# Weight chunks of a hybrid decoder layer: low parts by ScalarE's negative and an accumulating DMA, low-part matmuls at the end of each tile

## The chip, the cores and the metric

The kernel runs on one core of one Trainium2 chip. The metric is the device time in microseconds (us) of one execution.

## What is computed

The reference is one decoder layer on 512 tokens of width 1024, in float32. A conditioned norm gives `h`; one wide GEMM `z = h @ w_in` feeds three causal mixers, whose outputs are projected up, gated and merged; a squared-ReLU MLP follows.

```python
h = rms_norm(x, g_norm1[l]) * (1.0 + sc1) + sh1
x = x + gt1 * hybrid_mixer(h, w_in[l], ...)
h = rms_norm(x, g_norm2[l]) * (1.0 + sc2) + sh2
x = x + gt2 * (jnp.square(jax.nn.relu(h @ w_mlp1[l])) @ w_mlp2[l])
...
z = h @ w_in
merged = jax.nn.sigmoid(ga) * y_a + jax.nn.sigmoid(gbr) * y_b + jax.nn.sigmoid(gc) * y_c
return merged @ w_out
```

`y_a` is a gated MLP over chunks of 128 tokens, `y_b` a matrix memory with forget gates (mLSTM), `y_c` a sparse attention of eight heads with a compressed, a selected and a window branch, each times its projection up.

## The kernel before, in words

Every GEMM runs in split precision. A float32 operand is written as the exact sum of a high and a low part, both of type float32r, and a product takes three matmuls: high by high, low by high, high by low. The rows of activations are split once (`hh`, `hl`), the weights stream.

Weights come in chunks of 128 partitions by up to 1024 columns (512 KB). `chunk` (line 105) loads one by a DMA that SyncE issues (SP in the profile) into `w_raw` (three buffers), ScalarE (ACT) rounds it to `w_hi` (line 109, two buffers), and one engine subtracts, `w_lo = w_raw - w_hi` (line 110, two buffers): GpSimd (POOL) where `pool_lo` is true, VectorE (DVE) elsewhere. So the low part of a chunk goes into the buffer that the chunk two places earlier has used.

```python
raw = load(src, cols)
hi = stream.tile([P, D], F32R, name="w_hi", tag="hi")[:, :cols]
lo = stream.tile([P, D], F32R, name="w_lo", tag="lo")[:, :cols]
V.tensor_copy(hi, raw) if dve_hi else A.copy(hi, raw)
(G if pool_lo else V).tensor_tensor(lo, raw, f(hi), op=ALU.subtract)
```

`pool_lo` is true for 53 chunks: the 8 of 768 columns of the first GEMM (lines 193 to 254), 2 column tiles of compressed keys and values and 3 chunks of small columns (two of 864 columns, one of 576; lines 415 to 422), the 12 of `early_fill` (lines 851 to 894), 12 for each of two calls of `merge` (8 gate tiles of `zt`, 4 of the projection up; lines 822 to 850) and 4 for the output gate of the mLSTM (`ztok`, lines 289 to 306). 84 others go by DVE.

The program has these stages. In the first (to about 64 us) the shift and scale of the norm are made: `early_mod` (line 202) loads rows of the modulation weights, `ada_raw`, and reduces them, three quarters on DVE (line 210) and one on POOL (line 207) with ACT; `early_h` (line 218) makes a column tile of `h`. The first GEMM takes the tiles as they come: for each of 8 chunks 6 matmuls of `w_hi` by `hh`, then 6 pairs of `w_hi` by `hl` and `w_lo` by `hh` (lines 244 to 254). Then come the compressed keys, the small columns and, from about 96 us, `early_fill`. The attention (about 125 to 256 us) is an order written out by hand for TensorE (PE), ACT and DVE, in which a step of `early_fill` follows each block of scores. From 256 us the gated MLP runs beside the first merge, until about 480 us the mLSTM beside two merges, and after that no chunk has `pool_lo`. Outside the stretches written by hand a scheduler orders each engine's queue from its own estimate of times.

`mm3` (line 113) issues the three matmuls of a pair of tiles one after the other, so that a low weight part is read at every third matmul (`L114`, `L115`, `L116`). `zt` makes a column tile of `z` from one chunk (24 matmuls of 512 columns), `ztok` a token block from two (48 of 256 columns each).

Of the kernel before, what the change touches and what calls it, by code (L numbers as in the profile page):

```python
# [11 lines left out]
ALU = mybir.AluOpType  # L12
# [30 lines left out]
# columns of the per-partition vector pack  # L43
V_C, V_G1, V_G2, V_SH1, V_SC1, V_SH2, V_SC2, V_CB, V_CW, V_PEK, V_PEV, V_LNG, V_LNB, V_NG, V_N = (
    0, 8, 16, 24, 32, 40, 48, 56, 64, 96, 128, 160, 164, 168, 172)
# columns of the row pack that is broadcast over the partitions
R_GB, R_BS = 0, 8
# order of the column tiles that are computed transposed
# [12 lines left out]
def trunk_kernel(ctx: ExitStack, tc: tile.TileContext, x, vecs, rows, late_rows, ada1, w_ada,  # L61
# [15 lines left out]
    def page(tag, name, dt=F32, width=S):  # L77
        """a tile of 512 columns (and a little) that outlives the step that writes it"""
        t = work.tile([P, 520 if tag == "kv" else S], dt, name=name, tag=tag, bufs=SLOTS[tag])
        return t[:, :width]  # L80
# [10 lines left out]
    def split(hi, lo, src, scale=None):  # L91
        """src (times scale) as the exact sum of two float32r parts"""
# [12 lines left out]
    def chunk(src, cols=D, pool_lo=False, dve_hi=False):  # L105
# [4 lines left out]
        (G if pool_lo else V).tensor_tensor(lo, raw, f(hi), op=ALU.subtract)  # L110
# [6 lines left out]

    def rstd_of(ss, n, name, scale=1.0 / D):
        """1/sqrt(ss*scale + EPS)"""
        r = small.tile([P, n], F32, name=name)  # L120
        V.tensor_scalar(r, ss, scale, EPS, op0=ALU.mult, op1=ALU.add)
        G.tensor_tensor(r, r, mhalf[:, 0:r.shape[1]], op=ALU.pow)
        return r
# [4 lines left out]
    # ---------------------------------------------------------------- loads and constants of the start  # L128
# [24 lines left out]
    # the condition as a row on all partitions  # L153
# [7 lines left out]
    # ---------------------------------------------------------------- first norm, transposed and split  # L161
# [20 lines left out]
    # 1/rms of the tokens as a row on all partitions  # L182
# [9 lines left out]
    def early_mod(j):  # L192
        """shift and scale of a column tile: the first by the tensor engine, the others along rows of the
        transposed weights"""
# [61 lines left out]
    # ---------------------------------------------------------------- constants of the mixers  # L256
# [23 lines left out]
    # ---------------------------------------------------------------- GEMM helpers on h^T  # L280
    def zt(n, pool_lo=False, tag="mm"):
        """column tile n of z, transposed: [128 columns, S]"""
        wh, wl = chunk(w_zt[n], D, pool_lo)
        ps = bank(tag, "zt")
        for k in range(KD):
            mm3(ps, wh[:, tsl(k)], wl[:, tsl(k)], hh[k], hl[k], k == 0, k == KD - 1)
        return ps

    def ztok(n, evac, pool_lo=True):
        """256 columns of z in token layout: two banks of two blocks; a step for each chunk of weights"""  # L290
        ps = [bank("mm", "ztok") for _ in range(2)]
        for c in range(2):
            wh, wl = chunk(w_tok[n * 2 + c], D, pool_lo)
            for tb in range(NT):
                o = ps[tb // 2][:, (tb % 2) * 256:(tb % 2) * 256 + 256]
                for kk in range(4):
                    k = 4 * c + kk
                    ws_ = slice(kk * 256, (kk + 1) * 256)
                    T.matmul(o, hh[k][:, tsl(tb)], wh[:, ws_], start=k == 0 and tb % 2 == 0, stop=False)
                    T.matmul(o, hl[k][:, tsl(tb)], wh[:, ws_], start=False, stop=False)  # L300
                    T.matmul(o, hh[k][:, tsl(tb)], wl[:, ws_], start=False, stop=k == KD - 1 and tb % 2 == 1)
# [6 lines left out]
    # ---------------------------------------------------------------- NSA operands  # L308
# [32 lines left out]
    # compressed keys and values: the windows, gathered by pairs of positions  # L341
    vc = []
    # per group: 32 columns of the high parts, 32 of the low ones
# [20 lines left out]
    def halves(name, src, eng):  # L364
        """16 blocks of 64 columns, each beside its rest: both float32r parts in one operand of 128 columns"""
# [42 lines left out]
    # values of the two dense branches, mLSTM gates, NSA gates: token layout  # L408
# [6 lines left out]
    for c, (k0, k1) in enumerate(((0, 3), (3, 6), (6, 8))):  # L415
        wh, wl = chunk(w_small[:, k0 * 288:k1 * 288], (k1 - k0) * 288, pool_lo=True)
        for tb in range(NT):
            for k in range(k0, k1):
                ws_ = slice((k - k0) * 288, (k - k0 + 1) * 288)
                T.matmul(sm[tb][:, :288], hh[k][:, tsl(tb)], wh[:, ws_], start=k == 0, stop=False)  # L420
                T.matmul(sm[tb][:, :288], hl[k][:, tsl(tb)], wh[:, ws_], start=False, stop=False)
                T.matmul(sm[tb][:, :288], hh[k][:, tsl(tb)], wl[:, ws_], start=False, stop=k == KD - 1)
# [11 lines left out]
    # ---------------------------------------------------------------- NSA attention  # L434
# [4 lines left out]
    def cmp_scores(g):  # L439
        """scores and weights of the compressed branch for the four heads of group g, in steps"""  # L440
# [43 lines left out]
    def scores(n, tb):  # L484
        """a block of rows of the scores, their bias and their maximum"""
# [24 lines left out]
    def scale(n, t0, t1):  # L510
        """exp(s - max) of blocks t0 to t1 times gate / sum"""
# [10 lines left out]
    def turn(n, sb):  # L522
        """the weights of a block of keys, transposed"""
# [14 lines left out]
    def apply(n, sb):  # L538
        """values of a block of keys times their weights"""
# [32 lines left out]
    # ---------------------------------------------------------------- gMLP  # L572
# [12 lines left out]
    def gelu2(ts):  # L585
        """twice the gelu, in place"""
# [45 lines left out]
    # ---------------------------------------------------------------- mLSTM  # L632
    bias_t = const.tile([P, 10, 4], F32, name="d_bias")
    em = const.tile([P, NT, 4], F32, name="em")
    # a row per head, the low parts 32 rows below the high ones
# [5 lines left out]
    def mlstm_gates():  # L641
# [23 lines left out]
        # sums of the log forget gates within blocks of 128, the running stabilizer  # L665
# [37 lines left out]
    def evac_mv(half):  # L703
        def ev(tb, ps):
            # two heads to a page: high part, one, zero, low part
# [14 lines left out]
    def conv(i, ps):  # L720
        """column tile i of q and k after the conv, silu and scale: two float32r parts"""
# [99 lines left out]
    # ---------------------------------------------------------------- merge of the gated branches  # L821
# [3 lines left out]
    def merge(b, yh, yl):  # L825
        """adds branch b of the three, two column tiles at a time: gates, then the projection up"""
# [531 lines left out]
```

## Time and profile before

| what | value |
|---|---|
| median of 3 runs | 973.5 us (972.73 to 974.67) |
| span of the profiled execution | 973.2 us, 0.3 us below the median |
| PE busy | 933.4 us, 96% |
| DVE, ACT, POOL busy | 612.2, 402.4, 193.7 us |
| DMA engines, queue of SP | 35.0% of 16 engines' span, 110.91 MB |

The profile gives no time of its own for the profiled execution beside its span. It lists, for each engine, groups of instructions by line of the kernel with their count, busy time and mean duration, the idle time before them and what ended it. Matmuls overlap: one of 512 columns shows about 0.39 us, and the next starts 0.23 us later. The granted clock is the share of TensorE's full speed (2.4 GHz) that was granted; 0.5 of it is the lower of two levels (1.2 GHz).

### The profile page before, as it was taken

The page shows a single profiled execution, that of the slowest core. Times are in us where ns is not written, and L with a number is a line of the kernel's source. Part 1 is how long each engine was busy: PE and PEld are TensorE (multiplying, and loading weights), DVE is VectorE, ACT ScalarE, POOL GpSimd, SP SyncE. Part 2 cuts the span into 40 slices and gives each one's busy share as a digit, 9 for nine tenths or more (in the row PEclk, how much of TensorE's full clock was granted, in tenths as well). Part 3 has the DMA queues.
Part 4 walks back from the last instruction along what each step waited for, and adds up shares of the span by engine and source line. Part 5 has one row for each costly group of instructions (what it writes and reads, how often), then busy time and mean ns, then how long its engine had stood idle before and what let it go on. Part 6 is the DMA issues. An engine that isn't in the chain of part 4 may idle for free.

```text
span 973.2 us, 12531 instructions
## 1 busy us (share of the span) xinstructions
PE 933.4 (96%) x4688; PEld 778.5 (80%) x4688; DVE 612.2 (63%) x1186; ACT 402.4 (41%) x789; POOL 193.7 (20%) x130
## 2 busy tenths in 40 slices
PE   7789998998979999999999999999999999999996
PEld 5569986797867888888977778888888888888886
DVE  6977679776497456556688799766424254442435
ACT  5355565765533444443333344544321223432221
POOL 5565423333343122123300003000000000000001
PEclk9899999998999999999999999999999999999998
DMA  9733210110222222222568864354333333223222
GB/s 328 229 118 116 66 44 26 40 44 26 84 65 87 87 86 88 70 82 89 172 211 274 258 251 119 92 182 128 94 100 91 104 89 107 87 89 106 87 87 87
DMA packets 36285, 111.72 MB, mean 115 GB/s; under 512 B 4160, under 2 KB 4352, under 8 KB 36224
## 3 DMA queue, kind: packets, MB, share of 16 engines
q1 hardware_dynamic: 36224, 110.91, 35.0%
q8 instruction: 37, 0.61, 0.3%
q14 instruction: 24, 0.20, 0.1%
HBM read 108.80 MB, written 2.10 MB: 114 GB/s over the span
## 4 chain that ended last, share of the span: by engine, by line
PE 75%; DVE 15%; DMA 6%; issue 2%; ACT 1%; SPq 0%; POOL 0%; POOLq 0%; DVEq 0%; ACTq 0%
PE tok L1086 6%; PE tok L1088 6%; PE tok L1087 6%; PE m L114 6%; PE m L116 6%; PE m L115 6%; PE zt L116 5%; PE zt L114 5%; PE zt L115 5%; DMA ada_raw<-in_w_ada 4%; DVE ada_raw L210 2%; PE pv L553 2%; PE pT L528 2%; PE ztok L887 2%; PE ztok L886 2%
## 5 line engine op out<-in xcount | busy, mean ns | idle before, releaser
L109 ACT CAST w_hi<-w_raw 128x1024 fp32r<-128x1024 f32 (+2 forms) x137 | 141.4, 1032 | 256.6 <-PE tok L1087 98.0
L110 DVE TENSOR_TENSOR w_lo<-w_raw,w_hi 128x1024 fp32r<-128x1024 f32 x84 | 103.8, 1236 | 171.1 <-ACT w_hi L109 171.1
L110 POOL TENSOR_TENSOR w_lo<-w_raw,w_hi 128x1024 fp32r<-128x1024 f32 (+3 forms) x53 | 125.1, 2360 | 242.9 <-ACT w_hi L109 240.3
L116 PE MATMUL zt<-h_hi,w_lo 128*128 128x512 f32 x304 | 121.1, 398 | 4.0 <-POOL w_lo L110 2.3
L114 PE MATMUL zt<-h_hi,w_hi 128*128 128x512 f32 x304 | 122.3, 402 | 0.5 <-ACT w_hi L109 0.5
L115 PE MATMUL zt<-h_lo,w_hi 128*128 128x512 f32 x304 | 119.9, 394 | 0.0
L114 PE MATMUL m<-h_hi,w_hi 128*128 128x512 f32 (+1 forms) x272 | 104.1, 383 | 0.0
L116 PE MATMUL m<-h_hi,w_lo 128*128 128x512 f32 (+1 forms) x272 | 103.7, 381 | 0.0
L115 PE MATMUL m<-h_lo,w_hi 128*128 128x512 f32 (+1 forms) x272 | 103.6, 381 | 0.0
L1087 PE MATMUL tok<-w_hi,f_lo 128*128 128x512 f32 (+1 forms) x232 | 88.6, 382 | 0.0
L1086 PE MATMUL tok<-w_hi,f_hi 128*128 128x512 f32 (+1 forms) x232 | 88.6, 382 | 0.0
L1088 PE MATMUL tok<-w_lo,f_hi 128*128 128x512 f32 (+1 forms) x232 | 84.4, 382 | 0.0
L116 PEld LDWEIGHTS zt<-h_hi,w_lo 128*128 128x128 f32 x304 | 57.6, 190 | 17.3 <-DVE w_lo L110 2.8
L114 PEld LDWEIGHTS zt<-h_hi,w_hi 128*128 128x128 f32 x304 | 57.6, 189 | 12.1 <-ACT w_hi L109 0.7
L115 PEld LDWEIGHTS zt<-h_lo,w_hi 128*128 128x128 f32 x304 | 57.6, 190 | 10.7
L1228 POOL TENSOR_TENSOR o_g<-x,gfin 128x512 f32<-128x512 f32 x1 | 1.3, 1297 | 311.0 <-DVE x L1132 311.0
L115 PEld LDWEIGHTS m<-h_lo,w_hi 128*128 128x128 f32 x272 | 51.2, 188 | 10.8
L116 PEld LDWEIGHTS m<-h_hi,w_lo 128*128 128x128 f32 x272 | 51.1, 188 | 10.8
L114 PEld LDWEIGHTS m<-h_hi,w_hi 128*128 128x128 f32 x272 | 51.1, 188 | 10.7
L1087 PEld LDWEIGHTS tok<-w_hi,f_lo 128*128 128x128 f32 x232 | 43.6, 188 | 8.6
L1086 PEld LDWEIGHTS tok<-w_hi,f_hi 128*128 128x128 f32 x232 | 43.6, 188 | 8.5
L1088 PEld LDWEIGHTS tok<-w_lo,f_hi 128*128 128x128 f32 x232 | 43.6, 188 | 8.4
(390 smaller groups left out, 2022.3 us busy)
## 6 DMA issues: line engine op xcount, KB each, us to landing
w_raw<-in_w_m SPq DMA_DIRECT2D x64, 512.0 KB, 3.5
w_raw<-in_w_zt SPq DMA_DIRECT2D x38, 512.0 KB, 3.3
ada_raw<-in_w_ada SPq DMA_DIRECT2D x24, 512.0 KB, 5.1
ada_raw<-in_ada SPq DMA_DIRECT2D x32, 256.0 KB, 4.9
w_raw<-in_w_tok SPq DMA_DIRECT2D x12, 512.0 KB, 3.3
w_raw<-in_w_up SPq DMA_DIRECT2D x12, 512.0 KB, 3.5
w_raw<-in_w_out SPq DMA_DIRECT2D x8, 512.0 KB, 4.8
w_raw<-in_w_ada SPq DMA_DIRECT2D x8, 512.0 KB, 3.9
```

Of the source, the lines that this page charges most:

```text
L109: V.tensor_copy(hi, raw) if dve_hi else A.copy(hi, raw)
L110: (G if pool_lo else V).tensor_tensor(lo, raw, f(hi), op=ALU.subtract)
L114: T.matmul(ps, ah, bh, start=first, stop=False)
L115: T.matmul(ps, ah, bl, start=False, stop=False)
L116: T.matmul(ps, al, bh, start=False, stop=last)
L210: V.scalar_tensor_tensor(raws[q], raws[q], 1.0, condb[:, (q % 2) * 512:(q % 2) * 512 + 512], op0=ALU.mult, op1=ALU.mult, accum_out=s4[:, q ...
L528: T.transpose(tp[:, tsl(tb)], sb_[:, boff(tb) + c0:boff(tb) + c0 + P], ident)
L553: T.matmul(acc[:, c0:], vv, p_[:, c0:], start=False, stop=last and p_ is t[-1])
L886: T.matmul(o, hh[k][:, tsl(tb)], wh[:, ws_], start=k == 0 and tb % 2 == 0, stop=False)
L1086: T.matmul(p_, ah_, wh, start=k == 0, stop=False)
L1087: T.matmul(p_, al_, wh, start=False, stop=False)
L1088: T.matmul(p_, ah_, wl, start=False, stop=k == 2 * n - 1)
```

## The change

Where `pool_lo` is true, `w_lo` is no longer a subtraction on POOL. ACT writes the negative of `w_hi` into `w_lo`, and POOL issues a DMA that adds the weights from DRAM to it. `w_raw` is then read by ACT alone, and the same weights are read from DRAM twice. `mm_hi` is new; in `zt`, `ztok`, the small columns, `merge` and `early_fill` the matmuls that read `w_lo` come after all those of the tile that read `w_hi` (in `merge` for both column tiles of a chunk, whose two banks are now taken together). The pairs of the first GEMM stay as they were. In `early_fill` the evacuation of the first bank pair moves to the last sixth of the second chunk. Comments and docstrings are gone, so lines are numbered anew.

```diff
@@ chunk
-        (G if pool_lo else V).tensor_tensor(lo, raw, f(hi), op=ALU.subtract)
+        if pool_lo:
+            A.activation(lo, f(hi), AF.Copy, scale=-1.0)
+            G.dma_start(lo, src, accum_op=ALU.add)
+        else:
+            V.tensor_tensor(lo, raw, f(hi), op=ALU.subtract)
+    def mm_hi(ps, ah, bh, bl, first):
+        T.matmul(ps, ah, bh, start=first, stop=False)
+        T.matmul(ps, ah, bl, start=False, stop=False)
@@ zt
         for k in range(KD):
-            mm3(ps, wh[:, tsl(k)], wl[:, tsl(k)], hh[k], hl[k], k == 0, k == KD - 1)
+            mm_hi(ps, wh[:, tsl(k)], hh[k], hl[k], k == 0)
+        for k in range(KD):
+            T.matmul(ps, wl[:, tsl(k)], hh[k], start=False, stop=k == KD - 1)
...
@@ merge
             wh, wl = chunk(w_up[b][jp], D, pool_lo)
+            ups = [bank(UP_BANK[b][u], "up") for u in range(2)]
+            for u in range(2):
+                for k in range(4):
+                    mm_hi(ups[u], wh[:, tsl(u * 4 + k)], yh[k], yl[k], k == 0)
             for u in range(2):
                 j = 2 * jp + u
-                ps = bank(UP_BANK[b][u], "up")
+                ps = ups[u]
                 for k in range(4):
-                    mm3(ps, wh[:, tsl(u * 4 + k)], wl[:, tsl(u * 4 + k)], yh[k], yl[k], k == 0, k == 3)
+                    T.matmul(ps, wl[:, tsl(u * 4 + k)], yh[k], start=False, stop=k == 3)
...
@@ early_fill
-                for k in range(KD):
-                    mm3(ps, wh[:, tsl(k)], wl[:, tsl(k)], hh[k], hl[k], k == 0, k == KD - 1)
-                    if k < KD - 1:
+                mms = [(wh, k, o) for k in range(KD) for o in (hh, hl)] + [(wl, k, hh) for k in range(KD)]
+                for n_, (w_, k, o) in enumerate(mms):
+                    T.matmul(ps, w_[:, tsl(k)], o[k], start=n_ == 0, stop=n_ == len(mms) - 1)
+                    if n_ % 3 == 2 and n_ < len(mms) - 1:
                         yield
...
```

`ztok`, the small columns and the token units of `early_fill` are rewritten in the same way. Three places show how the queues move. In the rows the names carry buffer numbers.

POOL's queue in the first stage, before:

```order
L110 TENSOR_TENSOR w_lo_219<-w_raw_216,w_hi_218 128x768
L207 TENSOR_TENSOR ada_raw_259<-ada_raw_259,condb_119 128x512
L110 TENSOR_TENSOR w_lo_268<-w_raw_265,w_hi_267 128x768
L207 TENSOR_TENSOR ada_raw_308<-ada_raw_308,condb_119 128x512
L110 TENSOR_TENSOR w_lo_317<-w_raw_314,w_hi_316 128x768
L207 TENSOR_TENSOR ada_raw_357<-ada_raw_357,condb_119 128x512
```

and the same place of POOL's queue now:

```order
L113 DMA w_lo_219<-in_w_early 128x768
L217 TENSOR_TENSOR ada_raw_260<-ada_raw_260,condb_119 128x512
L113 DMA w_lo_269<-in_w_early 128x768
L217 TENSOR_TENSOR ada_raw_310<-ada_raw_310,condb_119 128x512
L217 TENSOR_TENSOR ada_raw_360<-ada_raw_360,condb_119 128x512
L113 DMA w_lo_319<-in_w_early 128x768
```

Each subtraction has become the issue of a DMA; the third chunk's issue has moved behind a further product of the modulation.

ACT's queue in the first stage, before, from the second chunk on:

```order
L109 CAST w_hi_267<-w_raw_265 128x768
L208 ACTIVATE ada_raw_259,ada_s_271<-ada_raw_259 128x512
L109 CAST w_hi_316<-w_raw_314 128x768
L232 ACTIVATE h_hi_289<-h_tmp_288,ab_285 128x512
L208 ACTIVATE ada_raw_308,ada_s_320<-ada_raw_308 128x512
L232 ACTIVATE h_hi_338<-h_tmp_337,ab_334 128x512
L208 ACTIVATE ada_raw_357,ada_s_369<-ada_raw_357 128x512
L109 CAST w_hi_365<-w_raw_363 128x768
```

and the same place now:

```order
L109 CAST w_hi_268<-w_raw_266 128x768
L112 ACTIVATE w_lo_269<-w_hi_268 128x768
L218 ACTIVATE ada_raw_260,ada_s_273<-ada_raw_260 128x512
L242 ACTIVATE h_hi_291<-h_tmp_290,ab_287 128x512
L218 ACTIVATE ada_raw_310,ada_s_323<-ada_raw_310 128x512
L242 ACTIVATE h_hi_341<-h_tmp_340,ab_337 128x512
L218 ACTIVATE ada_raw_360,ada_s_373<-ada_raw_360 128x512
L109 CAST w_hi_318<-w_raw_316 128x768
L112 ACTIVATE w_lo_319<-w_hi_318 128x768
```

Behind each rounding stands the pass that writes the negative, and the third chunk's rounding has moved behind the tiles `h_hi` of the second and third column.

PE's queue in the first merge, before, with `up` the projection up:

```order
L114 MATMUL up_3037<-yc_hi_1780,w_hi_3033 128x512
L115 MATMUL up_3037<-yc_lo_1781,w_hi_3033 128x512
L116 MATMUL up_3037<-yc_hi_1780,w_lo_3034 128x512
L114 MATMUL up_3037<-yc_hi_2139,w_hi_3033 128x512
L115 MATMUL up_3037<-yc_lo_2140,w_hi_3033 128x512
L116 MATMUL up_3037<-yc_hi_2139,w_lo_3034 128x512
```

and the same chunk now, where 16 matmuls of `w_hi` for both column tiles end and 8 of `w_lo` begin:

```order
L125 MATMUL up_3066<-yc_hi_2586,w_hi_3060 128x512
L126 MATMUL up_3066<-yc_lo_2587,w_hi_3060 128x512
L125 MATMUL up_3066<-yc_hi_2872,w_hi_3060 128x512
L126 MATMUL up_3066<-yc_lo_2873,w_hi_3060 128x512
L863 MATMUL up_3065<-yc_hi_1800,w_lo_3061 128x512
L863 MATMUL up_3065<-yc_hi_2161,w_lo_3061 128x512
L863 MATMUL up_3065<-yc_hi_2586,w_lo_3061 128x512
```

The first reader of `w_lo` has moved from the third matmul of a chunk to the seventeenth.

## Rows read from the trace of the kernel before

**Rows 1.** The page, busy time of each engine with its share and count.

```profile
PE 933.4 (96%) x4688; PEld 778.5 (80%) x4688; DVE 612.2 (63%) x1186; ACT 402.4 (41%) x789; POOL 193.7 (20%) x130
```

**Rows 2.** Stretches: length, busy time by engine, granted clock, DMA share, GB/s.

```profile
12.00:64.00 52.00, 41.82 (x160) 30.79 (x160) 46.50 (x85) 18.55 (x34) 28.81 (x18) 0.87 0.68 235
140.00:256.00 116.00, 108.64 (x650) 92.55 (x650) 81.01 (x243) 69.95 (x192) 34.95 (x22) 0.97 0.10 33
256.00:302.00 46.00, 40.80 (x184) 32.14 (x182) 42.39 (x66) 23.10 (x40) 21.04 (x10) 0.93 0.29 92
302.00:480.00 178.00, 178.00 (x922) 151.53 (x922) 104.23 (x194) 73.63 (x144) 47.12 (x21) 1.00 0.27 89
```

**Rows 3.** Waits of PE over the span: us in total, times, longest us.

```profile
PE early L249 <- ACT h_hi L232: 7.9, 4, 4.8
PE pT L528 <- DVE scores L518: 7.3, 8, 2.4
...
PE zt L116 <- POOL w_lo L110: 2.3, 1, 2.3
```

**Rows 4.** Timeline of DVE, first stage: start us, duration us, instruction.

```profile
18.56 0.69 DVE L210 SCALAR_TENSOR_TENSOR ada_raw<-ada_raw,condb 128x512 f32<-128x512 f32 x1
...
21.55 2.32 DVE L210 SCALAR_TENSOR_TENSOR ada_raw<-ada_raw,condb 128x512 f32<-128x512 f32 x1
...
30.19 0.15 DVE L213 TENSOR_TENSOR ada_s<-ada_s 128x2 f32<-128x2 f32 x1
```

**Rows 5.** Timeline of POOL at the same place.

```profile
21.04 2.29 POOL L110 TENSOR_TENSOR w_lo<-w_raw,w_hi 128x768 fp32r<-128x768 f32 x1
```

**Rows 6.** Timeline of DVE in the attention, one tiny product twice.

```profile
166.99 2.08 DVE L515 TENSOR_TENSOR sums<-sums,gate 128x2 f32<-128x2 f32 x1
...
175.38 0.16 DVE L515 TENSOR_TENSOR sums<-sums,gate 128x2 f32<-128x2 f32 x1
```

**Rows 7.** Timeline of POOL at the first of them.

```profile
166.65 2.40 POOL L110 TENSOR_TENSOR w_lo<-w_raw,w_hi 128x1024 fp32r<-128x1024 f32 x1 [3.67 <-ACT w_hi L109]
```

**Rows 8.** The tile w_lo: POOL's subtraction, duration ns least, median, most.

```profile
L110 POOL TENSOR_TENSOR w_lo<-w_raw,w_hi x53: 1416/2395/3042, 15.0 to 472.1; 128x1024 fp32r<-128x1024 f32 x42, 128x768 fp32r<-128x768 f32 x8, 128x864 fp32r<-128x864 f32 x2, 128x576 fp32r<-128x576 f32 x1
```

**Rows 9.** Groups of DVE by form, first stage: count, busy us, mean ns.

```profile
L210 DVE SCALAR_TENSOR_TENSOR ada_raw<-ada_raw,condb 128x512 f32<-128x512 f32 x21 | 24.7, 1203 | 0.6 <-ACT condb L243 0.6
...
L213 DVE TENSOR_TENSOR ada_s<-ada_s 128x2 f32<-128x2 f32 x7 | 4.3, 608 | 0.0
```

**Rows 10.** Groups of POOL by form in the first stage.

```profile
L110 POOL TENSOR_TENSOR w_lo<-w_raw,w_hi 128x768 fp32r<-128x768 f32 x8 | 16.2, 2028 | 16.5 <-ACT w_hi L109 16.5
...
L207 POOL TENSOR_TENSOR ada_raw<-ada_raw,condb 128x512 f32<-128x512 f32 x7 | 11.7, 1672 | 2.9 <-ACT condb L243 2.9
```

**Rows 11.** Timeline of PE, first GEMM, first matmuls of the second and last chunk.

```profile
28.11 2.92 PE L249 MATMUL early<-h_hi,w_hi 128*128 128x512 f32 x6 [4.76 <-ACT h_hi L232]
...
63.55 1.52 PE L249 MATMUL early<-h_hi,w_hi 128*128 128x512 f32 x6
```

**Rows 12.** Groups of ACT by form: the rounding of weight chunks.

```profile
L109 ACT CAST w_hi<-w_raw 128x1024 fp32r<-128x1024 f32 x126 | 132.3, 1050 | 249.2 <-PE tok L1087 98.0 <-PE m L115 66.5 <-PE zt L115 39.1
...
L109 ACT CAST w_hi<-w_raw 128x768 fp32r<-128x768 f32 x8 | 6.6, 830 | 7.3 <-DMA w_raw<-in_w_early 2.5 <-DMA ada_raw<-in_ada 2.3 <-issue 1.4
```

**Rows 13.** Timeline of PE in a merge, two matmuls that are 24 apart.

```profile
380.02 0.39 PE L116 MATMUL zt<-h_hi,w_lo 128*128 128x512 f32 x1
...
385.46 0.39 PE L116 MATMUL zt<-h_hi,w_lo 128*128 128x512 f32 x1
```

**Rows 14.** DMA issues: count, KB each, median us from issue to landing.

```profile
w_raw<-in_w_zt SPq DMA_DIRECT2D x38, 512.0 KB, 3.3
...
w_raw<-in_w_early SPq DMA_DIRECT2D x8, 384.0 KB, 5.3
```

**Rows 15.** POOL's instructions of line 110 alone, by stretch: length, busy us (count).

```profile
140.00:256.00 116.00, 19.33 (x9) 0.97 0.10 33
256.00:302.00 46.00, 17.39 (x7) 0.93 0.29 92
```

More of the change, by code (lines that the diff above doesn't have):

```diff
@@ L293, in ztok @@
             wh, wl = chunk(w_tok[n * 2 + c], D, pool_lo)
-            for tb in range(NT):
+            for tb, kk in [(tb, kk) for tb in range(NT) for kk in range(4)]:
                 o = ps[tb // 2][:, (tb % 2) * 256:(tb % 2) * 256 + 256]
[L296 to L301, printed above, removed]
+                k = 4 * c + kk
+                ws_ = slice(kk * 256, (kk + 1) * 256)
+                T.matmul(o, hh[k][:, tsl(tb)], wh[:, ws_], start=k == 0 and tb % 2 == 0, stop=False)
+                T.matmul(o, hl[k][:, tsl(tb)], wh[:, ws_], start=False, stop=False)
+            for tb, kk in [(tb, kk) for tb in range(NT) for kk in range(4)]:
+                o = ps[tb // 2][:, (tb % 2) * 256:(tb % 2) * 256 + 256]
+                k = 4 * c + kk
+                T.matmul(o, hh[k][:, tsl(tb)], wl[:, kk * 256:(kk + 1) * 256], start=False,
+                         stop=k == KD - 1 and tb % 2 == 1)
             if c == 0:
@@ L421, in trunk_kernel @@
                 T.matmul(sm[tb][:, :288], hl[k][:, tsl(tb)], wh[:, ws_], start=False, stop=False)
+        for tb in range(NT):
+            for k in range(k0, k1):
+                ws_ = slice((k - k0) * 288, (k - k0 + 1) * 288)
                 T.matmul(sm[tb][:, :288], hh[k][:, tsl(tb)], wl[:, ws_], start=False, stop=k == KD - 1)
@@ L880, in early_fill @@
                 ps = [bank("mm", "ztok") for _ in range(2)]
-            for tb in range(NT):
+            mms = [(tb, kk, a_, wh) for tb in range(NT) for kk in range(4) for a_ in (hh, hl)]
+            mms += [(tb, kk, hh, wl) for tb in range(NT) for kk in range(4)]
+            for n_, (tb, kk, a_, w_) in enumerate(mms):
+                k = 4 * c + kk
                 o = ps[tb // 2][:, (tb % 2) * 256:(tb % 2) * 256 + 256]
-                for kk in range(4):
-                    k = 4 * c + kk
-                    ws_ = slice(kk * 256, (kk + 1) * 256)
-                    T.matmul(o, hh[k][:, tsl(tb)], wh[:, ws_], start=k == 0 and tb % 2 == 0, stop=False)
-                    T.matmul(o, hl[k][:, tsl(tb)], wh[:, ws_], start=False, stop=False)
-                    T.matmul(o, hh[k][:, tsl(tb)], wl[:, ws_], start=False, stop=k == KD - 1 and tb % 2 == 1)
-                    if kk == 1 or (kk == 3 and (c == 0 or tb % 2 == 0)):
-                        yield
-                if c == 1 and tb % 2 == 1:
+                T.matmul(o, a_[k][:, tsl(tb)], w_[:, kk * 256:(kk + 1) * 256],
+                         start=k == 0 and tb % 2 == 0 and a_ is hh and w_ is wh,
+                         stop=k == KD - 1 and tb % 2 == 1 and w_ is wl)
+                if c == 1 and w_ is wl and kk == 3 and tb % 2 == 1:
                     ev = (evac_gv(0), evac_gv(1), evac_mv(0), evac_mv(1))[n]
@@ L894, in early_fill @@
                         ev(t_, ps[t_ // 2][:, (t_ % 2) * 256:(t_ % 2) * 256 + 256])
+                if n_ % 6 == 5:
                     yield
```

## The prediction

> **What bounds the kernel now.** I read the busy time first. PE works for 96% of the span [rows 1], so anything that shortens other engines counts only where PE stands idle or runs at a reduced clock, and anything that makes PE wait counts in full. The stretches show where that is [rows 2]. From 302 to 480 us PE is busy for all 178 us at full clock: nothing can be gained there, only lost. From 12 to 64 us PE is idle for 52.00 - 41.82 = 10.2 us and its granted clock is 0.87; DVE is busy for 46.50 of the 52 us, and PE's longest waits are for a tile of `h` [rows 3], which DVE makes. In the attention, 140 to 256 us, PE is idle for 7.4 us, about what it waits for DVE's scaled scores (7.3 us) [rows 2, 3]. From 256 to 302 us it is idle for 5.2 us, and the clock of 0.93 takes another 0.07 x 46 = 3.2 us, while DVE is busy for 42.39 of 46 us.
>
> Then I asked what slows DVE in those three stretches. In the first, one product takes 0.69 us alone and 2.32 us when it starts half a microsecond after a subtraction of POOL, which ends with it [rows 4, 5]. In the attention a product of 128x2 takes 0.16 us alone, and 2.08 us when POOL's subtraction has just begun [rows 6, 7]. So DVE is held until POOL's instruction is over. That is what the change removes: 53 such instructions, of median 2.4 us [rows 8].
>
> **First stage (8 chunks).** DVE's line 210 averages 1.203 against 0.69 us, an excess of 21 x 0.51 = 10.8 us; line 213 averages 0.608 against 0.15 us, 7 x 0.46 = 3.2 us [rows 9, 4]. Together 14 us. POOL had 16.2 us of subtractions and 11.7 us of products of line 207 there [rows 10], and the products stay; the subtractions' share, 16.2 / 27.9, is 8 us, or 1.2 us per chunk. Six chunks take PE from 28.11 to 63.55 us, 5.9 us each [rows 11]. DVE alone would let it be 4.7 us.
>
> The new path of a low part may not allow that. Its buffer is free when PE ends the chunk two places earlier. Then ACT rounds and negates (0.83 us each [rows 12], the second priced as the first), POOL issues the DMA, and it lands after X; PE then still has its 12 paired matmuls, 12 x 0.227 = 2.7 us (24 matmuls start within 5.44 us [rows 13]). Two chunks thus take at least 1.7 + X + 2.7 us. No row shows an adding DMA. The lower bound for X is a plain load of the same chunk, 5.3 us [rows 14], since the same bytes come from DRAM; the upper one is two such loads, 10.6 us, as the destination must be read as well. These loads are slow because the queue is full (share 0.68, 235 GB/s [rows 2]), so I stay nearer the lower end: 393 KB more at 300 GB/s, a round figure above that rate, is 1.3 us, X = 6.6. Then a chunk takes 5.5 us, 0.4 us less than now, and 7 of them gain **3 us**. At 5.3 us the limit is 4.85 us and the gain 7 us; at 10.6 us it is 7.5 us, a loss of 11 us.
>
> **Attention (9 chunks [rows 15]).** Most of POOL's subtractions hold up DVE where PE has other work; some put off a scaled block of scores. The bounds are 0 and the 7.3 us of [rows 3]. I take **2 us**, the size of one such hold [rows 6], because ACT, in an order written by hand, gets a pass of 1.05 us more per chunk [rows 12] at 60% load [rows 2], and the additions of the attention output stay on POOL. A chunk lasts over 10 us here (9 in 116 us), so X is covered.
>
> **Gated MLP (7 chunks [rows 15], 256 to 302 us).** DVE paces PE. Seven holds of up to 1.9 us [rows 6] are 13 us of DVE, but PE lost only 5.2 + 3.2 = 8.4 us. Between 0 and 8.4 I take **5 us**: over half, since DVE is the bound there, and not all, since POOL's own power of the variances stays and ACT gets seven passes.
>
> **PE-bound stretches (64 to 140 and 302 to 480 us).** With the low parts last, the need for `w_lo` moves from the third to the seventeenth matmul of a chunk. From the release of its buffer PE runs one whole chunk, 5.44 us, and two thirds of the next, 3.6 us: 9.1 us. ACT's negative takes 1.05 us and some 0.2 us of handing over, which leaves **7.8 us for X**. Bounds for 512 KB: one plain load, 3.3 us [rows 14], and three (source, destination, write back one after the other), 9.9 us. I take the middle, two loads, 6.6 us, since two reads are needed and the queue is light (share 0.27 [rows 2]). It is covered. ACT's queue is in order, and a pass behind a wait comes late now and then; PE waited 2.3 us once for a low part of POOL [rows 3], so I charge **2 us** more. The added passes (53 of about 1 us on ACT's 402 us [rows 1]) and the loads, 26 MB, are hidden behind PE as long as X is; without that cover, see the first rival. The reading of `w_raw` by one engine fewer costs and gives nothing: the loads are ahead of the rounding already.
>
> The sum: -3 - 2 - 5 + 2 = -8 us. The profiled span of 973.2 us lies 0.3 us below the median, so I set it against the median: 973.5 - 8 = **965.5 us**. With the bounds of the terms above this case reaches from 951 (7 + 7 + 8 us gained, no charge) to 972 us.
>
> One page prices the DMA. The Trainium skill ("DMA: Bandwidth & Descriptors", section "Anatomy of one DMA — SWDGE (gpsimd) path") gives about 2.0 us plus the bytes at 436 GB/s for one issued by GpSimd. With the bytes counted twice for the two reads I estimate 4.4 us for 512 KB and 3.8 us for 384 KB from that page; no run here shows it. By it the first stage would be paced by DVE and gain 8 us, the charge of 2 us would fall away, and the sum would be -15 us, 958.5 us.
>
> **The rivals.** (1) *The adding DMA lands later than PE can wait.* It decides from X = 7.8 us in the PE-bound stretches. Two chunks then take at least 1.25 + X + 8 x 0.227 = 3.1 + X us instead of 10.9. At the upper bound, X = 9.9 us, that is 1.05 us per chunk; with 53 - 8 - 9 - 7 = 29 chunks there 30 us. The first stage loses 11 us with its own upper bound, and the gains of 7 us elsewhere remain: 973.5 + 30 + 11 - 7 = 1007.5 us. For it: no row shows such a DMA, and PE's granted clock falls where it stands idle often (0.87 in the first stage [rows 2]), which would add. Against: light queues, and a scheduler that puts other matmuls between. (2) *Only the first stage suffers*, its queue being full: X of 10 us there gives (4.4 + 10) / 2 = 7.2 us per chunk and 7 x 1.3 = 9 us lost; the other parts are -2 - 5 + 2: about 977.5 us. It decides from X = 7.4 us. (3) *DVE's holds were not what PE waited for*, since POOL's remaining products and ACT's new passes hold as long; the parts cancel, 973 us. (4) *POOL is held by DVE when it issues.* Its subtractions reach 3.04 us against a median of 2.395 [rows 8], so up to 0.65 us of holding shows now; put on X it gives 7.25 us, still covered, and on the first stage 0.3 us per chunk: some 4 us of the 8 remain, 969.5 us. A rule speaks for it and against the change: the Trainium skill ("SBUF — State Buffer", section "Summary: rules for kernel authors") has descriptor generation on GpSimd starved while DVE runs in its faster modes. The trace has no DMA of POOL to show it. (5) *The parts aren't moved*: excluded, the queues show the new rows.
>
> **How the numbers follow.** The forecast gets 0.44: the holds are plainly in the trace, and X = 6.6 us lies 1.2 us inside the limit. Rival 1 gets 0.30, as its bound lies only 2 us above the limit; rival 2 0.12; rival 3 0.09; rival 4 0.05. A measurement of this kernel tells apart about 0.2%, 2 us. Faster: 0.44 + 0.05 = 0.49; the same: 0.09; slower: 0.30 + 0.12 = 0.42. Cases of both signs hold most of the chance, so the forecast's own range, 951 to 972 us, stands beside the wide one. That reaches from 952 to 1010 us, a little past rival 1 at its bound; about 0.15 lies above, where X is longer still, and little below.
>
> **What would show it.** In the changed kernel's profile the issue-to-landing time of `w_lo` decides: under 7.8 us and no waits of PE for a DMA of `w_lo` bears me out. DVE's line 210 should fall to about 0.9 us on average, the product of 128x2 to 0.2 us, and PE be idle less than 3 us from 256 to 302 us. PE waits in the merges for `w_lo`, with a lower granted clock there, would show rival 1; waits in the first GEMM alone, rival 2.

## The result and the profile after

The changed kernel takes 986.9 us (median; 985.7 to 990.7), the kernel before 973.5 us: a ratio of 1.0127, with a 95% interval of 1.0103 to 1.0151. That is 13 us slower, where 8 us faster was forecast. The profiled execution has a span of 984.2 us, 11.0 us more than before.

First the stretches that answer to [rows 2]; the columns are the same.

```profile
12.00:64.00 52.00, 38.82 (x145) 27.98 (x145) 37.17 (x85) 23.04 (x39) 17.27 (x17) 0.87 0.92 274
64.00:140.00 76.00, 66.55 (x435) 60.30 (x434) 38.15 (x119) 47.17 (x84) 20.90 (x20) 0.98 0.66 153
140.00:256.00 116.00, 113.69 (x694) 96.68 (x694) 84.20 (x286) 83.97 (x218) 24.58 (x22) 1.00 0.38 82
256.00:302.00 46.00, 40.80 (x201) 33.81 (x200) 21.82 (x46) 26.65 (x49) 7.82 (x9) 0.93 0.59 137
302.00:480.00 178.00, 177.26 (x885) 148.04 (x884) 97.66 (x195) 96.72 (x166) 17.62 (x20) 1.00 0.59 141
```

The second of these stretches was, before:

```profile
64.00:140.00 76.00, 75.80 (x526) 70.23 (x525) 54.75 (x165) 46.99 (x104) 38.10 (x21) 1.00 0.27 86
```

Until 140 us PE is busy for less now: 38.8 of 52 us (41.8 before) and 66.6 of 76 us (75.8 before), although DVE and POOL have less to do. In the attention it is busy for more, at full clock. The waits of PE say why (they answer to [rows 3]):

```profile
PE early L264 <- DMA w_lo<-in_w_early: 13.4, 6, 4.4
PE zt L298 <- DMA w_lo<-in_w_zt: 7.6, 4, 4.7
PE sm L440 <- DMA w_lo<-in_w_small: 5.7, 2, 3.4
...
PE pT L546 <- DVE scores L536: 0.4, 1, 0.4
```

The wait for the scores, 7.3 us before, is down to 0.4 us. In place of it PE waits 26.7 us for adding DMAs. Their times, from the list of DMA issues (count, KB each, median us from issue to landing):

```profile
w_lo<-in_w_zt POOLq DMA_DIRECT2D x22, 512.0 KB, 5.5
...
w_lo<-in_w_tok POOLq DMA_DIRECT2D x12, 512.0 KB, 5.6
...
w_lo<-in_w_early POOLq DMA_DIRECT2D x8, 384.0 KB, 7.0
```

So the median X was 5.5 us where 6.6 was taken, and 7.0 us in the first stage where 6.6 was taken: both inside the limits that the prediction worked out (7.8 and 7.4 us). The price was about right, and the kernel is slower all the same.

To see where the time went I cut each trace at matmuls that mark the same place of the program: the first and the last of `early`, the last of `sm` (small columns), the first of `pT` (attention), the last of `up` of the first merge, the first of `m` (squared-ReLU MLP). Such starts stand in the view of a tile (duration min/median/max in ns, then first and last start in us), here for the changed kernel:

```profile
L259 PE MATMUL early<-h_hi,w_hi x48: 387/390/838, 20.8 to 71.1; 128*128 128x512 f32 x48
...
L264 PE MATMUL early<-h_hi,w_lo x48: 387/393/795, 24.4 to 74.2; 128*128 128x512 f32 x48
```

Each cell of the table is a difference of two starts, in us, from one profiled execution each; the names of the runs are those of the experiments below.

| kernel | first GEMM | to end of small columns | to attention | attention and first merge | to the MLP |
|---|---|---|---|---|---|
| before | 48.8 | 28.1 | 24.8 | 225.1 | 263.7 |
| changed | 53.4 | 35.1 | 27.0 | 220.7 | 263.3 |
| early_by_subtraction | 48.8 | 34.9 | 26.0 | 219.8 | 261.7 |
| first13_by_subtraction | 50.0 | 28.5 | 27.3 | 220.7 | 261.7 |
| order_alone | 49.9 | 28.6 | 26.3 | 224.1 | 261.6 |
| plain_dma_in_place_of_adding | 49.6 | 33.5 | 25.5 | 215.7 | 261.8 |
| dma_in_early_fill_only | 50.3 | 28.9 | 27.1 | 215.3 | 262.0 |
| dma_in_first_merge_only | 48.5 | 28.9 | 26.3 | 230.3 | 260.2 |
| fill_only_again | 50.4 | 28.8 | 27.5 | 215.2 | 260.6 |
| fill_and_first_merge_less_two | 48.9 | 28.9 | 27.3 | 212.3 | 258.6 |

Of the 11 us the first GEMM has 4.6 and the stretch to the end of the small columns 7.0; the attention with the first merge gives back 4.4. The first matmul of the GEMM comes at 20.8 us instead of 18.6, but it does so in `order_alone` too, which changes nothing ahead of it (19.9 to 22.1 us over the experiments): so the adding DMA does not make these 2.2 us.

### The profile page after: what moved, and what is told of

The parts are those of the page before. It is cut to its first block, busy times and chain, and to the rows that moved or that the text cites. A ratio compares the mean times of both kernels' runs of the same rounds, so it can differ in the third digit from the quotient of the medians.

```text
span 984.2 us, 12612 instructions
## 1 busy us (share of the span) xinstructions
PE 934.1 (95%) x4688; PEld 779.3 (79%) x4688; DVE 565.5 (57%) x1186; ACT 452.2 (46%) x842; POOL 112.8 (11%) x130
## 3 DMA queue, kind: packets, MB, share of 16 engines
q0 software_dynamic: 7632, 26.35, 16.2%
## 4 chain that ended last, share of the span: by engine, by line
PE 77%; DMA 10%; DVE 6%; issue 4%; ACT 2%; POOL 1%; SPq 0%; POOLq 0%; DVEq 0%; ACTq 0%
PE tok L1109 7%; PE tok L1110 7%; PE tok L1111 7%; PE m L121 6%; PE m L120 6%; PE m L119 6%; PE zt L298 5%; PE zt L125 5%; PE zt L126 5%; PE ztok L910 4%; DMA w_lo<-in_w_zt 3%; DMA ada_raw<-in_ada 2%; PE up L125 2%; PE up L126 2%; PE pv L571 2%
## 5 line engine op out<-in xcount | busy, mean ns | idle before, releaser
L125 PE MATMUL zt<-h_hi,w_hi 128*128 128x512 f32 x272 | 107.6, 395 | 0.5 <-DVE mv L95 0.5
L126 PE MATMUL zt<-h_lo,w_hi 128*128 128x512 f32 x272 | 106.6, 392 | 0.0
L298 PE MATMUL zt<-h_hi,w_lo 128*128 128x512 f32 x272 | 71.1, 401 | 7.7 <-DMA w_lo<-in_w_zt 7.6
L298 PEld LDWEIGHTS zt<-h_hi,w_lo 128*128 128x128 f32 x272 | 51.5, 192 | 20.1 <-DMA w_lo<-in_w_zt 9.5
L125 PEld LDWEIGHTS zt<-h_hi,w_hi 128*128 128x128 f32 x272 | 51.4, 189 | 11.5 <-PE pv L571 0.7
L112 ACT ACTIVATE w_lo<-w_hi 128x1024 fp32r<-128x1024 f32 (+3 forms) x53 | 53.8, 1014 | 13.3 <-PE zt L298 5.9
L126 PEld LDWEIGHTS zt<-h_lo,w_hi 128*128 128x128 f32 x272 | 51.3, 189 | 10.2
L94 ACT CAST f_hi<-relu 128x512 fp32r<-128x512 f32 x32 | 19.9, 621 | 41.8 <-DVE relu L1278 41.8
```

The source lines that it names most:

```text
L112: A.activation(lo, f(hi), AF.Copy, scale=-1.0)
L125: T.matmul(ps, ah, bh, start=first, stop=False)
L126: T.matmul(ps, ah, bl, start=False, stop=False)
L298: T.matmul(ps, wl[:, tsl(k)], hh[k], start=False, stop=k == KD - 1)
```

## Experiments

My theory (A) was that the adding DMA is too late in stages that use up a chunk faster than the chain of buffer, negative and DMA allows, that is, for the first 13 chunks; the rival (B) that the new order of the matmuls costs. Runs 1 to 4 were measured together on one chip, and so were runs 5 and 7 to 9, runs 6, 10 and 11, and runs 12 to 15. The kernel before ran beside each group, with medians of 974.6 to 975.7 us; ratios are to it.

**1. `early_by_subtraction`**

```diff
-        ws_early[j] = chunk(w_early[j], 768, pool_lo=True)
+        ws_early[j] = chunk(w_early[j], 768, pool_lo="sub")
```

Here and below `"sub"` stands for the subtraction on GpSimd, as in the kernel before.

> The 8 chunks of the first GEMM go back to the subtraction on GpSimd; the other 45 keep the adding DMA. Theory A (the adding DMA lands too late for stages in which a chunk is used up faster than its chain of buffer, negative, DMA): the first GEMM begins and ends as in the kernel before, 6.8 us earlier than in the changed kernel, and the rest of the loss stays: 986.9 - 6.8 = 980 us. Theory B (the loss is the new order of the matmuls): the first GEMM was not reordered, so its 6.8 us were something else and the time stays near 987 us. Rival: what the first GEMM gains is lost again in the stage after it, 986 us.

Measured: 980.7 us, ratio 1.0057 (1.0033 to 1.0081). The first GEMM is back at 48.8 us and nothing else moves (table).

**2. `first13_by_subtraction`**: the same for the `zt` of compressed keys and values and the three chunks of small columns.

> As the first, and also the 2 chunks of compressed keys and values and the 3 of small columns by subtraction; their low-part matmuls stay last. Theory A: the 7.0 us lost between the first GEMM and the end of the small columns go too, and the gains in the attention (1.9 us) and beside the gated MLP (3.7 us) remain: 986.9 - 6.8 - 7.0 = 973 us, and 971 us if the 2.2 us ahead of the attention go as well. Theory B (order): the small columns stay late, 978 us or more.

Measured: 974.1 us, ratio 0.9981 (0.9960 to 1.0001). The small columns end 28.5 us after the GEMM, as before. Together the 13 chunks cost 12.8 us, nearly all of the loss.

**3. `order_alone`**

```diff
-            A.activation(lo, f(hi), AF.Copy, scale=-1.0)
-            G.dma_start(lo, src, accum_op=ALU.add)
+            G.tensor_tensor(lo, raw, f(hi), op=ALU.subtract)
```

> All 53 chunks by subtraction on GpSimd, only the order of the matmuls is the changed kernel's. Theory A: the order costs and gains nothing, 973.5 us within 2 us, with VectorE's product of the modulation held to 1.2 us on average as before. Theory B: the order costs most of the 13 us, 980 us or more.

Measured: 975.1 us, ratio 0.9992 (0.9970 to 1.0014). B falls: the order by itself is worth nothing. PE waits 7.5 us for the scores here, as before.

**4. `plain_dma_in_place_of_adding`**

```diff
-            G.dma_start(lo, src, accum_op=ALU.add)
+            G.dma_start(lo, src.bitcast(F32R))
```

> GpSimd's DMA copies the weights into the low part and does not add (what is left out: the subtraction, so the low part is the weight itself). Same negative, same waits, same queue. If reading and writing back the destination makes the DMA long, issue to landing falls from 5.5 us to about 3.5 us, SyncE's plain load of 512 KB, PE's waits for it in the first 110 us mostly go, and the time is about 977 us. If the path from GpSimd makes it long, it stays at 5 us or more and the time within 2 us of 986.9 us.

This kernel leaves out the addition; its bytes and its order of instructions are the changed kernel's. Measured: 971.7 us, ratio 0.9957 (0.9934 to 0.9981), 5 us below what was expected. GpSimd's plain DMA lands after 3.7 to 4.5 us (`zt`, `tok`), 1.1 to 1.8 us sooner than the adding one. The page's list of queues, of the changed kernel and then of this one (packets, MB, share of 16 engines' span), shows what the adding takes:

```profile
q0 software_dynamic: 7632, 26.35, 16.2%
```

```profile
q0 software_dynamic: 7632, 26.35, 8.9%
```

It keeps the DMA engines busy 1.8 times as long for the same 26.35 MB. So the adding itself costs 15 us here. It is not all that hurts: PE's waits for low parts halve, from 26.7 to 14.0 us, and do not go, and 971.7 us is not the forecast's 965.5 even with X at 4 us. In the stretch to the end of the small columns (33.5 us) PE still waits 3.7 us for `sm`.

**5. `first_gemm_low_last`**

```diff
             for i in range(6):
                 T.matmul(early[i], wh[:, tsl(i)], hl[j], start=False, stop=False)
+            for i in range(6):
                 T.matmul(early[i], wl[:, tsl(i)], hh[j], start=False, stop=j == KD - 1)
```

> The changed kernel, with the six low-part matmuls of each chunk of the first GEMM after the other twelve. Theory A1 (the chain buffer, negative, DMA paces the first GEMM): two chunks then take at least 1.7 + X + 6 matmuls (1.4 us) in place of 12 (2.7 us), 0.67 us less per chunk; the 4.6 us lost in the first GEMM go, 982 us, and PE's 13.4 us of waits for these DMAs fall to under half. Theory A2 (the negative is late because ScalarE's queue is in order and stands behind tiles of h that wait for VectorE): the DMA lands as late as before and the time stays near 987 us.

Measured: 984.7 us, ratio 1.0106 (1.0084 to 1.0129). PE's waits there fall only from 13.4 to 10.4 us, the longest is 5.0, and the first GEMM takes 54.3 us. A1, the prediction's own formula, isn't borne out: 982 us and waits under half were expected by it.

**6. `first_gemm_scalar_order`**

```diff
-    with tc.manual_schedule(engines={mybir.EngineType.PE}):
+    with tc.manual_schedule(engines={mybir.EngineType.PE, mybir.EngineType.Activation}):
         early_mod(0)
```

> The changed kernel, with ScalarE's queue in the first stage in program order, so that the rounding and the negative of a chunk stand ahead of the tile h of the same column. Theory A2 (the DMA is issued late because of ScalarE's queue): PE's waits for the first GEMM's DMAs, 13.4 us, fall below 7 us, and the time to 983 us. If the DMA itself (7.0 us from issue to landing there) sets the pace, the waits stay over 10 us and the time at 987 us within 2 us; if ScalarE then holds up the tiles of h, PE waits for those instead and the time is 987 us or more.

Measured: 984.1 us, ratio 1.0086 (1.0061 to 1.0111). PE's waits, of this kernel:

```profile
PE sm L440 <- DMA w_lo<-in_w_small: 7.2, 2, 4.1
...
PE early L259 <- ACT h_hi L242: 6.1, 3, 2.1
PE early L264 <- DMA w_lo<-in_w_early: 4.9, 6, 1.6
```

The waits for the low part fall from 13.4 to 4.9 us and the first GEMM takes 49.8 us, 3.6 us less. A2 holds for most of these waits: ScalarE's queue was late. But PE now waits 6.1 us for `h` where it waited 0.6, and 2.9 us are given back in the stretch behind (38.0 us), which this edit leaves alone; the whole kernel gains 3 us.

**7. `dma_with_old_order`**: as 2, with `mm3` back in `zt` and in the projection up.

> As first13_by_subtraction (the DMA for the 40 later chunks), but zt and the projection up read high, high, low in turn as in the kernel before (early_fill and ztok keep the low part last). If the low-part matmuls at the end are what covers the DMA: the need for the low part falls back to the third matmul of a chunk, the limit for issue to landing from 7.8 to 4.6 us, below the 5.3 us measured; two chunks then take 1.25 + 5.3 + 22 x 0.227 = 11.55 us instead of 10.9, 0.33 us for each of 24 chunks of the merges: 974.1 + 8 = 982 us. Rival: the scheduler puts other matmuls between and it stays within 2 us of 974 us.

Measured: 1001.6 us, ratio 1.0268 (1.0239 to 1.0296), 27 us above run 2. PE waits for the low part 22.0 us in `zt` and 6.3 in `up`. So the order is worth nothing alone, and without it the DMA costs 27 us more. The loss is over three times the 8 us worked out from two chunks at a time; why it is so much larger stays open.

**8. `dma_in_early_fill_only`**: as 2, and all chunks of the merges and the output gate by subtraction.

> Only the 12 chunks of early_fill take the DMA, all others the subtraction; order of the matmuls as in the changed kernel. If the gain sits in the attention (VectorE's scores no longer held): PE's wait for the scores, 7.5 us with the order alone, falls under 1 us and the time is 973 us or less. If it sits beside the gated MLP, the time is that of the order alone, 975 us.

Measured: 965.9 us, ratio 0.9913 (0.9894 to 0.9933), 9 us below the order alone: the gain sits in the attention. PE's wait for the scores is 0.4 us.

**9. `dma_in_first_merge_only`**: as 2, with the DMA in the 12 chunks of the first merge alone.

> Only the 12 chunks of the first merge (beside the gated MLP) take the DMA. If the gain sits there, 973 us or less; if it sits in the attention, PE still waits 7 us for the scores and the time is 975 us or more, since two adding DMAs that overlap land after 9 us there.

Measured: 978.9 us, ratio 1.0046 (1.0031 to 1.0061), 4 us above the order alone. PE waits 5.1 us once for a low part that lands after 9.5 us. The DMA in the chain of waits (start, duration), and PE's next row:

```profile
267.75 9.53 DMA w_lo<-in_w_zt
```

```profile
277.33 3.78 PE L300 MATMUL zt<-h_hi,w_lo 128*128 128x512 f32 x8 [5.09 <-DMA w_lo<-in_w_zt]
```

Had it landed after this kernel's median of 5.3 us, 4.2 of the 5.1 us would have gone. The wait costs more than itself: from 277.3 to 287.0 us the granted clock is 0.70, where it was 1.00 in the 9.7 us up to 267.7. In the changed kernel the same DMA stands so:

```profile
270.76 9.09 DMA w_lo<-in_w_zt
```

**10. `fill_and_first_merge_less_one`**: as 8, with the DMA in the first merge too, but

```diff
-            wh, wl = chunk(w_up[b][jp], D, pool_lo)
+            wh, wl = chunk(w_up[b][jp], D, "sub" if pool_lo and jp == 0 else pool_lo)
```

> early_fill and the first merge take the DMA, except the merge's first chunk of the projection up, which is subtracted; all others subtracted. In earlier runs PE's one long wait in the first merge (4.7 to 5.1 us) is for a DMA that is issued 2.7 us behind that chunk's and lands after 9.1 to 9.5 us instead of 5.3. If two adding DMAs under way at once are the cause, no DMA lands after more than 7.5 us, the wait goes, and the time is that of dma_in_early_fill_only, 966 us within 2 us. If something else of the first merge costs the time (more passes on ScalarE, the loads beside it), a wait stays and the time is 969 us or more.

Measured: 970.9 us, ratio 0.9952 (0.9930 to 0.9973). One DMA still takes 8.4 us with no second adding DMA beside it, and PE waits 4.0 us for it. So two adding DMAs at once are not the cause. At the same moment SyncE loads `bsr` and `wst` for the gated MLP, and these are late too. The list of DMA issues of the changed kernel:

```profile
bsr<-in_rows SPq DMA_DIRECT2D x1, 256.0 KB, 7.8
...
wst<-in_ws_t SPq DMA_DIRECT2D x1, 256.0 KB, 10.2
```

In `order_alone` they take 4.0 and 4.2 us, in this run 6.5 and 6.7. With the plain DMA of run 4 they take 6.4 and 7.5: the loads are slowed by that one too, if by less.

**11. `fill_and_later_stages`**: as 8, with the DMA in the last merge and the output gate too.

> early_fill, the last merge with pool_lo and the output gate take the DMA, the first merge the subtraction. If the DMA is covered where PE is busy throughout (16 other matmuls ahead of each low part), the time is that of dma_in_early_fill_only, 966 us within 1.5 us. If these 16 chunks also cost (first13_by_subtraction was 8 us above early_fill alone, of which the long wait explains 5), 968 us or more.

Measured: 972.0 us, ratio 0.9964 (0.9946 to 0.9982). Its trace shows no wait for a low part in these stages but one of 0.2 us, so runs 12 to 14 take the stages apart.

**12 to 14.** **`fill_only_again`** is the kernel of run 8, **`fill_and_last_merge`** and **`fill_and_output_gate`** are the halves of run 11.

> dma_in_early_fill_only once more, beside the next three on one chip. If its gain is as measured, 0.991 of the kernel before, 966 us; if that chip was lucky, up to 0.995 (970 us).

> early_fill and the 12 chunks of the last merge with pool_lo by the DMA, the rest subtracted. If a covered DMA is free, the time is that of fill_only_again within 1.5 us. If these chunks cost, by later starts or a queue of ScalarE that holds up the conv and the gates, 3 us or more above it.

> early_fill and the 4 chunks of the output gate by the DMA, the rest subtracted. If free, within 1.5 us of fill_only_again. One tile takes two chunks here, so both low buffers are held to its end; if that costs, PE shows a wait at the output gate's low part and the time is 2 us or more above.

Measured: 967.4 us (0.9921, 0.9900 to 0.9941), 967.0 us (0.9914, 0.9894 to 0.9934) and 968.3 us (0.9933, 0.9910 to 0.9957). Both halves are free within what can be told apart. Their sum, run 11, was some 4 us dearer by ratio (0.9964 against 0.9921), on another chip. A part of it can be seen: in runs 11 and 14 PE waits 1.0 and 2.2 us for DVE's gate `sig` in the third merge, in run 12 not at all. The rest stays open.

**15. `fill_and_first_merge_less_two`**: as 10, and

```diff
-                ps = zt(ZT_SIG + b * 8 + 2 * jp + u, pool_lo, ZT_BANK.get((b, jp, u), "mm"))
+                ps = zt(ZT_SIG + b * 8 + 2 * jp + u, "sub" if pool_lo and (jp, u) == (1, 0) else pool_lo, ZT_BANK.get((b, jp, u), "mm"))
```

> As fill_and_first_merge_less_one, and the gate tile behind that chunk is subtracted too, so that no adding DMA is under way while bsr and wst load. If those loads beside the adding DMA make it land after 8 to 9 us, bsr and wst land after some 4 us again, no DMA takes more than 7 us, PE's wait of 4 to 5 us goes, and the time is that of fill_only_again or less by 1 to 3 us (less holding of VectorE). If a wait for a low part stays, the cause is ScalarE's late negative.

Measured: 963.1 us, ratio 0.9879 (0.9857 to 0.9901), the fastest of all. The longest adding DMA takes 7.4 us, a little over the 7 us expected. The loads land in time again, by the list of DMA issues:

```profile
bsr<-in_rows SPq DMA_DIRECT2D x1, 256.0 KB, 4.0
...
wst<-in_ws_t SPq DMA_DIRECT2D x1, 256.0 KB, 4.1
```

and from 258 to 304 us, the first 46 us of the merge, the stretches show for `dma_in_first_merge_only` (at the same place of the program), and then for this kernel:

```profile
267.00:313.00 46.00, 39.86 (x172) 31.68 (x171) 32.01 (x66) 29.44 (x50) 7.80 (x9) 0.93 0.68 166
```

```profile
258.00:304.00 46.00, 45.45 (x223) 36.96 (x222) 35.81 (x73) 31.12 (x52) 10.54 (x11) 1.00 0.69 172
```

PE is busy for 45.45 us instead of 39.86, and at full clock. So the cause is the adding DMA beside those loads. The two loads take 6.4 us or more in every run that has GpSimd's DMA at that moment and at most 4.2 us in every other, and the DMA engines were busy for 0.95 of the time from 267.7 to 277.3 us in run 9, 0.68 at the same place here. This run takes the DMA away; one that moves the two loads instead wasn't made.

## Why the prediction was wrong

**X, the DMA's time.** Right in size: 5.5 us against 6.6 taken for 512 KB, 7.0 against 6.6 for 384 KB. The bounds from the trace of before held for the medians; that the middle of such wide bounds was near is partly luck. The page of the Trainium skill that was weighed ("DMA: Bandwidth & Descriptors", "Anatomy of one DMA — SWDGE (gpsimd) path") gave an estimate of 4.4 us for 512 KB and 3.8 us for 384 KB with the bytes counted twice. For 512 KB it is as far from the measured 5.5 us as the 6.6 was, on the other side; for 384 KB, with 7.0 measured, it is far too low.

**First stage: -3 us forecast, +4.6 us in the trace, +6 us by run 1.** The step that failed is "Its buffer is free when PE ends the chunk two places earlier. Then ACT rounds and negates". ACT does so when its queue comes to it. For the later stretches the prediction charged 2 us for that, here nothing. The third chunk, in ACT's timeline of the changed kernel:

```profile
31.20 0.72 ACT L242 ACTIVATE h_hi<-h_tmp,ab 128x512 fp32r<-128x512 f32 x1 [2.79 <-DVE h_tmp L241]
...
32.44 0.82 ACT L109 CAST w_hi<-w_raw 128x768 fp32r<-128x768 f32 x1
33.28 0.84 ACT L112 ACTIVATE w_lo<-w_hi 128x768 fp32r<-128x768 f32 x1
```

then POOL's and PE's:

```profile
34.42 0.88 POOL L113 DMA_DIRECT2D w_lo<-in_w_early  x1 [6.26 <-DMA ada_raw<-in_ada]
```

```profile
42.22 0.80 PE L264 MATMUL early<-h_hi,w_lo 128*128 128x512 f32 x1 [4.42 <-DMA w_lo<-in_w_early]
```

(The view puts POOL's idle time down to a load; the issue comes 0.3 us behind the end of the negative, as at the other chunks.) PE had left the first chunk by 27.8 us, where it begins the second; the rounding comes at 32.4, behind a tile of `h` that waits for DVE. The next two chunks are the same: three waits, 9.3 of the 13.4 us, follow a rounding that comes 2.8 to 4.6 us late by this measure. From the rounding to the low part in use it is 9.8 us now, where before it was 0.8 for the rounding and some 2 for the subtraction [rows 5, 12]. A late rounding used to cost little; now all of X hangs behind it. The order rows ahead of the prediction showed this very rounding moving behind two tiles of `h`, and the sum made nothing of it. Runs 5 and 6 tell the two apart: later use of the low part gains little, an earlier negative takes away 8.5 of the 13.4 us of waits, of which waits for `h` take back 5.5.

The other half of this term, DVE's product, fell a little further than forecast (about 0.9 us was said). In [rows 4, 5] it ends 0.5 us after the subtraction, and not with it as the prediction has it, which changes no term. Now:

```profile
L220 DVE SCALAR_TENSOR_TENSOR ada_raw<-ada_raw,condb 128x512 f32<-128x512 f32 x21 | 16.0, 787 | 1.1 <-ACT condb L253 1.0
```

Yet no kernel's first GEMM got shorter than 48.5 us, and with the low part in time PE waits 6.1 us for `h` (run 6). The traces name what stands in DVE's place. POOL's remaining products still hold DVE, here a product of `h` that takes 0.75 us elsewhere:

```profile
34.54 3.88 DVE L241 SCALAR_TENSOR_TENSOR h_tmp<-xT,ab,rb 128x512 f32<-128x512 f32 x1
```

```profile
35.03 2.82 POOL L217 TENSOR_TENSOR ada_raw<-ada_raw,condb 128x512 f32<-128x512 f32 x2
```

And beside the added bytes the loads that `h` needs land later: the DMA engines' share from 12 to 64 us rises from 0.68 to 0.92, and the loads of `ada_raw` between 12 and 70 us land after 5.4 us (6.0 in run 6) instead of 4.3; in run 6 POOL waits 9.4 us for them. The prediction took the added loads as hidden. How much of the missing gain each of these explains, no run shows.

**"PE-bound stretches": +2 us forecast, +7.0 us in the trace, +6.6 us by run 2.** The sum put 64 to 140 us under one cadence with the merges, 5.44 us per chunk. In the small columns a chunk is 36 matmuls of 288 columns that start 0.13 us apart, 4.7 us, and in the first of these chunks only 12 of them, 1.6 us, run ahead of the low part. Of the timelines of PE, ACT and POOL:

```profile
81.66 1.98 PE L298 MATMUL zt<-h_hi,w_lo 128*128 128x512 f32 x8
...
91.49 1.05 PE L440 MATMUL sm<-w_lo,h_hi 128*128 128x288 f32 x6 [3.35 <-DMA w_lo<-in_w_small]
```

```profile
85.16 0.92 ACT L112 ACTIVATE w_lo<-w_hi 128x864 fp32r<-128x864 f32 x1
```

```profile
86.38 0.86 POOL L113 DMA_DIRECT2D w_lo<-in_w_small  x1 [5.47 <-ACT w_lo L112]
```

The buffer comes free when the eight matmuls from 81.66 end, at about 83.5; the low part is used at 91.5. These 8 us are the chain that was called covered at 9.1 us: 1.7 us until ACT comes to the negative, behind roundings of other tiles, 0.9 for the negative, 0.3 to the issue and 5.1 for the DMA. PE's other work in that time was the 12 matmuls and eight of the other `zt`, some 3.7 us. This is read from the trace; no run changes the cover there alone. In the merges after 302 us the cover held but for one wait of 0.7 us. Runs 13 and 14 put the cost there within 1 us of nothing, where 2 us were charged; run 11 put it at some 4 us.

**Attention: -2 us forecast, -7 to -9 us measured** (runs 8 and 12 against run 3, by ratio and by median). The mechanism was right and the size wrong: of the 7.3 us of waits for DVE's scores [rows 3] all but 0.4 went, and the granted clock rose from 0.97 to 1.00 over 116 us, by my estimate some 3 us more. The sum took one hold of [rows 6]; it should have taken the wait that the holds made.

**Gated MLP: -5 us forecast, +4 to +5 us measured** (run 9 against run 3, by median and by ratio). Missed was a step that the change doesn't touch: two loads of SyncE pass the DMA engines at that moment, and behind the wait that follows PE's granted clock is lower as well (run 9). Of the prediction's signs, PE idle for less than 3 us from 256 to 302 us failed: 5.2 us, as before. Without the DMA at that moment the part gains 4.3 us (run 15 against run 12), close to the forecast.

**The sum.** By the medians: the order +0.3 us against the kernel before, early_fill -9.2, the merges and the output gate +8.2 (run 2 less run 8), keys and small columns +6.6, the first GEMM +6.2. From 974.8 us that leads to 986.9, as it must, since each step starts at the run where the one before ended. Each step is uncertain by some 2 us, and more where its two runs were on different chips: of the 8.2 us of the merges the first merge alone explains 4 to 5, and runs 13 and 14 show no cost of the rest that can be told apart.

**The rivals.** The second, that only the first stage suffers, came nearest (977.5 us); it had the place of half the loss, but gave an X of 10 us as the reason, and X was 7.0. The first needs X above 7.8 us in the PE-bound stretches. The median stayed below; the low part came too late there all the same, because the chain started late and the cover was short, and in the first merge one DMA reached 9.1 us. The third falls for the attention with run 8; in the first stage, where POOL's products still hold DVE and `h` comes no sooner, it isn't excluded. The fourth has nothing for it: POOL's DMA issues take 0.85 to 1.08 us each, also from 20 to 50 us, where DVE is busy for 29 of 30 us. (Its sum was off: 0.3 us on 7 chunks leaves nearly 6 of the 8 us, not 4.) The rule that it drew on, of the Trainium skill ("SBUF — State Buffer", "Summary: rules for kernel authors"), is for DVE in its 2x or 4x mode. No view here shows an instruction's mode, so these runs don't test that rule.

## What to carry to other kernels

When an engine's pass is replaced by a DMA, work out the cover where the chunk is used, stage by stage, and start the chain at the place in the issuing queues where the first instruction really stands, not at the moment when its buffer is free. Price what an engine's holds cost by the wait that they end in, not by one hold. Then move only the chunks that have cover and no other loads on the DMA engines at that moment: the 22 of run 15 give 0.988 of the time before, all 53 give 1.013.

## What the runs showed of the hardware

An adding DMA from DRAM kept the DMA engines 1.8 times as busy as a plain one of the same bytes (16.2% against 8.9%) and landed 1.1 to 1.8 us later. Two loads of 256 KB beside it took 7.8 and 10.2 us instead of 4.0 and 4.2 (6.4 and 7.5 beside a plain one), and the adding DMA 9.1 instead of 5.5. A product of 128x512 on DVE took 3.88 us instead of 0.75 beside two products of POOL. After PE had stood idle for 5.1 us, the granted clock of the next 9.7 us was 0.70.
